# Pointwise product as the scan's last filler, two more pairs of input tiles by seven products

## The chip, the cores and the metric

One Trainium2 chip, one core. The metric is the device time of one execution in microseconds (us); lower is better. The chip's engines are called TensorE (PE in the profile; PEld is its weight load), VectorE (DVE), ScalarE (ACT), GpSimd (POOL) and SyncE (SP, which issues DMAs here).

## What is computed

One layer of a bidirectional sequence model, for 1024 positions of width 1024, in float32:

```
h = RMSNorm(x)
P = h @ W_in                     # 1024 x 8192 columns: GLU, q, v, z_f, z_b, og, g_a, g_b
a = GLU(P) -> depthwise conv (31) -> LayerNorm -> silu -> a @ W_pw      # 512 -> 1024
b = two gated scans (forward, backward) of q, v, z over 8 heads -> norm, gate -> @ W_o
x = x + W_out(sigmoid(g_a) * a + sigmoid(g_b) * b)
x = x + W_down(silu(dwconv3(h2 W_gate)) * (h2 W_up)),  h2 = RMSNorm(x)
return RMSNorm(x)
```

The change concerns the product `a @ W_pw` (the pointwise product), and four of the 64 column tiles of 128 that `h @ W_in` is made of.

## The kernel before, in words

Activations stand transposed: a tile has 128 channels on the partitions and 512 positions, half of the sequence. A tile of a product's output is 128 columns of the weight matrix times one half of the positions. Every factor is kept as a high and a low part (`split`, line 122: the cast to the high part is ScalarE's, the subtraction that leaves the low part is VectorE's, line 123), and a product of two such tiles takes three matmuls (`mm3`, lines 142 to 149: high by high, high by low, low by high). Weights are loaded into `wr` (2 buffers) and split into `wp` (4 pages); activations lie in `hx` (32 pages of 256 KB), and h itself takes 16 of those for each half of the positions.

There are three kinds of jobs. Each has a `prep`, which loads and splits its weights, and a `run`, which issues matmuls in pieces of six:

- `std_job` (line 250) computes one tile of 128 columns for one or both halves. With 8 contraction blocks, as for `h @ W_in`, that is 24 matmuls or 4 pieces a half; the pointwise product has 4 blocks, so 12 matmuls or 2 pieces a half.
- `duo_job` (line 267) takes two tiles together, first both on the first half, then both on the second.
- `pair_job` (line 281) computes two tiles of 128 columns over both halves by seven products of 12 matmuls in place of eight (Strassen's scheme). The sums of activations that it needs lie in `hx` and `hy` pages, the sums of weights are made from `wr` and `sw`, and part of its weight parts lie in `wq`, in the pool `p1`.

`run_jobs` (line 193) hands out the pieces of a list of jobs in order. The next job's `prep` is called when the one before has handed out its first pieces, and `later(n, do)` has something done n pieces later. A `Stream` wraps that: `fill(n)` issues n pieces at this point of the program. The program's order is therefore written by hand: what stands between two fills is issued between those pieces, on every engine.

The 56 tiles of `h @ W_in` that aren't the GLU's are in the list `todo`: per head q and og, then per head v, z_f, z_b, then the gates g_a and g_b. Their outputs are evicted by ScalarE and stored to DRAM scratch (`d_q`, `d_v`, `d_z`, `d_ga`, ...), from where later stages load them.

The stages around the change:

1. *Pairs* (lines 940 to 1010). The first 2 x NPAIRS = 34 entries of `todo` are computed as 17 pairs. They fill TensorE while VectorE makes the depthwise convolution (`conv_steps`, line 944) and then, once per half of the positions, the layer norm: it loads the convolved tiles from `d_cv` (line 978), sums over channels by matmuls with ones (lines 982, 518 and 528), and writes the normed, activated and split result to the tiles `ch` in the pool `gp0` (line 998).
2. *Pointwise product* (lines 1002 to 1010). After each half's layer norm 8 `std_job`s of that half are put into the list of jobs behind the pairs; 16 in all, 192 matmuls, reading `ch`. Each of the 16 loads and splits its weights anew. Then the pools `p1` and `gp0` are released.
3. *Scan* (lines 1015 to 1400). The pool `hp` takes their memory. `scan_inputs` (line 1053) loads z, q of a head and half and makes the gates on ScalarE and VectorE; `scan_base` (line 1077) forms cumulative products, with its tensor operations recorded by the helper at line 1042 (`DE`, `qF`, `kG`); `scan_levels`, `scan_states` and `scan_outputs` hold the scan's own, mostly small matmuls (lines 1162, 1174, 1188, 1245, 1295). Between them stand pieces of the 22 remaining entries of `todo` as filler, the stream `dense`: 21 pieces ahead of the first scan step, then `FILL` = 1.3 pieces between steps, and what is left after the last head in a fixed pattern (`left`, line 1403). The last filler job is a `duo_job` of the last two gate tiles. One v tile is loaded per head and half on SP (`load(d_v...)`), into the `tm` pages.
4. *Output of the scan.* `bm_loads` (line 1360) loads the scan's outputs from `d_bm` and splits them into `hx` pages, for the product with W_o. After that come the merge, W_out and the feed-forward part; the pointwise result is read back there from `d_a`.

Of the kernel before, what the change touches and what calls it, by code (L numbers as in the profile page):

```python
# [10 lines left out]
F32 = mybir.dt.float32  # L11
# [7 lines left out]
P = 128  # L19
FILL = 1.3  # L20
CONV_FILL = 1.6
NPAIRS = 17
LN_FILL = 6
LN_LAST = 12
GLU_FIRST = 4
# [21 lines left out]
def tile_hybrid_encoder(  # L47
# [22 lines left out]
    nc = tc.nc  # L70
    PSUM = bass.MemoryType.PSUM
    V, A, G, T = nc.vector, nc.scalar, nc.gpsimd, nc.tensor

    S, D = x.shape[1], x.shape[2]
    ND = D // P
    CW = conv_dw_w.shape[2]
    CK = conv_dw_w.shape[1]
    NCW = CW // P
# [20 lines left out]
    def bank(tag):  # L99
        return ps.tile([P, H], F32, tag=tag, name=nm(tag), bufs=BANKS[tag])  # L100

    def page(pool, tag, bufs, dt=F32):
        return pool.tile([P, H], dt, tag=tag, name=nm(tag), bufs=bufs)
# [4 lines left out]
    def ev():  # L108
        return page(mp, "ev", 3)

    def hx():
        return page(mp, "hx", 32, F32R)
# [9 lines left out]
    def split(hi, lo, src, eng, late=False):  # L122
        parts = A.copy(hi, src), eng.tensor_tensor(lo, src, hi.bitcast(F32), op=ALU.subtract)  # L123
        if late:
            for i in parts:
                pin(i)
        return hi, lo

    def w_cols(w, r0, nk, c0, cols=P):
        return w[0, r0 : r0 + nk * P, c0 : c0 + cols].rearrange("(k p) e -> p k e", p=P)  # L130

    def raw_w(src, nk):
        t = mp.tile([P, nk, P], F32, tag="wr", name=nm("wr"), bufs=2)
        nc.sync.dma_start(t, src)
        return t

    def w_page(nk, pool=None):
        if pool is None:
            return mp.tile([P, nk, P], F32R, tag="wp", name=nm("wp"), bufs=4)
        return pool.tile([P, nk, P], F32R, tag="wq", name=nm("wq"), bufs=3)  # L140

    def mm3(acc, w, act, k, first, last, again=False):


        whi, wlo = w
        ahi, alo = act
        T.matmul(acc, whi[:, k, :], ahi, start=first, stop=False, skip_group_check=again)  # L147
        T.matmul(acc, whi[:, k, :], alo, start=False, stop=False, skip_group_check=again)  # L148
        T.matmul(acc, wlo[:, k, :], ahi, start=False, stop=last, skip_group_check=again)  # L149
# [7 lines left out]
    def later(n, do):  # L157

        chores.append([n, do])

    def advance_chores(n=1):
        for c in list(chores):
            c[0] -= n
            if c[0] <= 0:
                chores.remove(c)
                c[1]()
# [26 lines left out]
    def run_jobs(jobs, lead=0, prime=0, first=None):  # L193


        live = collections.deque(maxlen=3)

        jobs = jobs if isinstance(jobs, collections.deque) else collections.deque(jobs)
        ready = collections.deque()

        def prepare(n):
            while jobs and len(ready) < n:
                prep, run = jobs.popleft()
                ready.append((run, prep()))
                live.append(ready[-1][1])

        def tick():
            for w in live:
                if isinstance(w, Weights):
                    w.tick()  # L210
            advance_chores()

        prepare(max(prime, 1))
        if prime:
            yield
        while ready:
            run, w = ready.popleft()
            pieces = run(w)
            for _ in itertools.islice(pieces, lead if first is None else first):
                tick()  # L220
                yield
            first = None
            prepare(1)
            for _ in pieces:
                tick()
                yield
            prepare(1)
# [21 lines left out]
    def std_job(src, nk, acts, evac, halves=(0, 1), step=2):  # L249


        def prep():
            raw = raw_w(src, nk)
            return split(w_page(nk), w_page(nk), raw, V)

        def run(w, halves=halves):
            for half in halves:
                acc = bank("mm")
                for k in range(nk):
                    mm3(acc, w, acts(k, half), k, k == 0, k == nk - 1)  # L260
                    if k % step == step - 1 or k == nk - 1:
                        yield
                evac(half, acc)

        return prep, run

    def duo_job(src0, src1, nk, acts, evac0, evac1):

        both = [std_job(src0, nk, acts, evac0), std_job(src1, nk, acts, evac1)]

        def prep():
            return [p() for p, _ in both]

        def run(w):
            for half in range(2):
                for (_, r), wi in zip(both, w):
                    yield from r(wi, (half,))

        return prep, run
# [197 lines left out]
    def scratch(name, *dims):  # L477
        if not dims:
            return dp.tile([P, H], F32, name=name)
        return [scratch(f"{name}_{i}", *dims[1:]) for i in range(dims[0])]  # L480

    d_h = scratch("d_h", ND, 2)
    d_cv = scratch("d_cv", NCW, 2)
    d_a = scratch("d_a", ND, 2)
    d_ga = scratch("d_ga", ND, 2)
    d_gb = scratch("d_gb", ND, 2)
# [12 lines left out]
    def in_cols(c0):  # L499
        return w_cols(w_in, 0, ND, c0)  # L500
# [212 lines left out]
    def store(dst, func=None):  # L713
        def evac(half, x0, x1=None, op=None):
            t = ev()
            if x1 is not None:
                V.tensor_tensor(t, x0, x1, op=op)  # L717
                x0 = t
            if func is not None:
                A.activation(t, x0, func)  # L720
            elif x1 is None:
                A.copy(t, x0)
            nc.sync.dma_start(dst[half], t)

        return evac
# [21 lines left out]
    def in_pair(n):  # L747
        (c0, e0), (c1, e1) = todo[2 * n], todo[2 * n + 1]
        evs = (e0, e1)
        return pair_job(  # L750
            in_cols(c0),
            in_cols(c1),
            NK2,
            lambda i: ht[i],
            p1,
            p1,
            lambda e, *quadrant: evs[e](*quadrant),
            first=n == 0 or n >= 12,
        )
# [179 lines left out]

    jobs = collections.deque(in_pair(n) for n in range(1, NPAIRS))  # L940
    jobs.appendleft((lambda: w_pair0, pair0[1]))
# [27 lines left out]
            V.tensor_tensor(o, o, t, op=ALU.add)  # L969
        return o  # L970

    pw_jobs = []
    for half in range(2):
        xs = []
        for j in range(NCW):
            if j % 2 == 0:
                both = p1.tile([P, 2, H], F32, tag="ca", name=nm("cx"), bufs=2)
            nc.sync.dma_start(both[:, j % 2, :], d_cv[j][half])
            xs.append(both[:, j % 2, :])
        s_pairs.fill(LN_FILL)  # L980
        mean = bank("ob")
        T.matmul(mean, ones_m, total(xs, tmp()), start=True, stop=True)
        for t in xs:
            V.scalar_tensor_tensor(t, mean, -1.0 / CW, t, op0=ALU.mult, op1=ALU.add)
        s_pairs.fill(LN_FILL)
        sqs = [tmp() for _ in xs]
        for sq, t in zip(sqs, xs):
            A.activation(sq, t, AF.Square)
        rstd = rstd_over_partitions(total(sqs, sqs[0]), CW, "ob", tmp())
        next(rstd)  # L990
        s_pairs.fill(5)
        rs = next(rstd)
        ca = []
        for j, xn in enumerate(xs):
            V.tensor_tensor(xn, xn, rs, op=ALU.mult)
            V.tensor_scalar(xn, xn, vec("lnw", j), vec("lnb", j), op0=ALU.mult, op1=ALU.add)
            A.activation(xn, xn, AF.Silu)
            both = gp0.tile([P, 2, H], F32R, tag="gl", name=nm("ch"), bufs=NCW)
            ca.append(split(both[:, 0, :], both[:, 1, :], xn, V))
        s_pairs.fill(LN_LAST)  # L1000
        at = 0
        while at < len(jobs) and jobs[at] in pw_jobs:
            at += 1
        for i in range(ND):
            job = std_job(
                w_cols(conv_pw_w, 0, NCW, i * P), NCW, lambda k, hf, ca=ca: ca[k], store(d_a[i]), (half,)
            )
            pw_jobs.append(job)
            jobs.insert(at + i, job)
    s_pairs.drain()  # L1010
    Stream(run_jobs(jobs)).drain()
    p1.release()
    gp0.release()


    rest = todo[2 * NPAIRS :]
    rest_jobs = [std_job(in_cols(c), ND, h_std, e) for c, e in rest[:-2]]
    (c0, e0), (c1, e1) = rest[-2:]
    rest_jobs.append(duo_job(in_cols(c0), in_cols(c1), ND, h_std, e0, e1))

    h12.clear()
    for k in range(NK2):
# [2 lines left out]
    dense = Stream(run_jobs(rest_jobs))  # L1025
# [343 lines left out]
    for h in range(NH):  # L1369
# [4 lines left out]
        for half in range(2):  # L1374
            i = 2 * h + half
# [24 lines left out]
            cur = ahead  # L1400
        pending = Stream(outputs(h, kept, Tt, Sf, Sb))

    left = 8 * (len(rest) - 2) + 16 - dense.count
    pending.fill(1)
    dense.fill(left - 20)
    pending.fill(1)
# [209 lines left out]
    gs, jobs = [], []  # L1616
# [183 lines left out]
```

## Time and profile before

| what | value |
|---|---|
| time, median of 3 runs (lowest, highest) | 1791.35 us (1791.15, 1793.52) |
| span of the profiled execution, first to last instruction | 1788.8 us |
| median less that span | 2.55 us |
| stages by start of TensorE's work in that trace: pairs | to 452.6 us |
| pointwise product | 452.6 to 500.6 us |
| filler ahead of the scan's first own matmul | 500.6 to 529.2 us |
| mean granted TensorE clock | 0.996 |

The profiled execution has no device time of its own beside the span; the span leaves out what the runs' times have around it. Times in the profile are counted from the span's start. In a row of the timeline the start, the duration, the engine, the source line, the operation, and output<-inputs by the program's names stand in this order; "x4" is a group of four, and a bracket tells the idle time before and what released it. A row "A <- B: 6.0, 7, 1.5" of the waits says that A stood 6.0 us for B in 7 waits, the longest 1.5.

### The profile page before, as it was taken

The numbers are of one execution on the slowest core, as the hardware profiler recorded it, in microseconds if no ns is written. First come the engines' busy times: TensorE is split into PE (matmuls) and PEld (weight loads), VectorE is DVE, ScalarE is ACT, GpSimd is POOL, SyncE is SP. The second block draws the span as 40 slices with busy tenths as digits, with TensorE's granted clock in tenths as the row PEclk, the third lists the DMA queues.
The fourth block names the chain that finished last, engine by engine and source line by source line (L and its number), as shares of the span: only waits on it lengthen the run. The fifth ranks groups of instructions, "written<-read, shape, count | busy, mean of one in ns | idle before, by whom it ended". The sixth has DMA issues, their size and how long they took to land.

```text
span 1788.8 us, 27583 instructions
## 1 busy us (share of the span) xinstructions
PE 1733.0 (97%) x10632; PEld 1416.7 (79%) x10638; DVE 1250.4 (70%) x1884; ACT 775.0 (43%) x1490; POOL 153.8 (9%) x168
## 2 busy tenths in 40 slices
PE   8989999999999999999999999999999999999997
PEld 6878877888777777777778888878888888888885
DVE  5599999746569999999645557667667667544455
ACT  7344333334555566655442245344344344422123
POOL 2201111000000000000000002011111111000000
PEclk9999999999999999999999999999999999999999
DMA  8657887743663433333257665567667665534233
GB/s 285 216 151 187 185 185 185 199 150 126 199 214 101 125 119 119 119 119 101 90 180 219 200 201 177 153 142 159 151 144 158 142 151 133 161 103 126 79 91 135
DMA packets 317705, 276.41 MB, mean 155 GB/s; under 512 B 14462, under 2 KB 242566, under 8 KB 317574
## 3 DMA queue, kind: packets, MB, share of 16 engines
q1 hardware_dynamic: 276406, 242.15, 43.1%
q0 software_dynamic: 41168, 32.51, 12.6%
q8 instruction: 83, 1.36, 0.3%
q14 instruction: 48, 0.39, 0.1%
HBM read 185.73 MB, written 72.61 MB: 144 GB/s over the span
## 4 chain that ended last, share of the span: by engine, by line
PE 65%; DVE 19%; DMA 5%; issue 4%; ACT 4%; POOL 1%; SPq 0%; POOLq 0%; DVEq 0%; ACTq 0%
PE mm L147 16%; PE mm L148 16%; PE mm L149 16%; PE sc L147 3%; PE sc L149 3%; PE sc L148 3%; DVE acc L955 2%; DVE kG L1042 2%; DVE DE L1042 2%; DVE qF L1042 2%; DVE wp L123 2%; PE tr L147 1%; PE tr L149 1%; PE tr L148 1%; DVE DE L1098 1%
## 5 line engine op out<-in xcount | busy, mean ns | idle before, releaser
L147 PE MATMUL mm<-hx,wp 128*128 128x512 f32 x1128 | 454.8, 403 | 9.8 <-DVE ev L717 4.3
L149 PE MATMUL mm<-hx,wp 128*128 128x512 f32 x1128 | 441.7, 392 | 1.9 <-DVE wp L123 1.9
L148 PE MATMUL mm<-hx,wp 128*128 128x512 f32 x1128 | 441.4, 391 | 0.0
L123 ACT CAST wp<-wr 128x1024 fp32r<-128x1024 f32 (+2 forms) x179 | 167.0, 934 | 359.6 <-PE mm L148 271.5
L147 PEld LDWEIGHTS mm<-hx,wp 128*128 128x128 f32 x1128 | 212.5, 188 | 55.7 <-DVE ev L717 6.7
L123 DVE TENSOR_TENSOR wp<-wr,wp 128x1024 fp32r<-128x1024 f32 (+2 forms) x177 | 191.4, 1082 | 90.4 <-ACT wp L123 90.1
L149 PEld LDWEIGHTS mm<-hx,wp 128*128 128x128 f32 x1128 | 212.6, 188 | 49.3 <-DVE wp L123 3.2
L148 PEld LDWEIGHTS mm<-hx,wp 128*128 128x128 f32 x1128 | 212.9, 189 | 40.4 <-issue 0.2
L955 DVE SCALAR_TENSOR_TENSOR acc<-gl,v_b,acc 128x1024 f32<-128x1024 f32 x120 | 149.0, 1277 | 0.5
L1651 DVE TENSOR_TENSOR xr<-mm,xr 128x512 f32<-128x512 f32 x48 | 33.2, 691 | 73.1 <-PE mm L149 73.1
L367 ACT COPY su<-mm 128x512 f32<-128x512 f32 x78 | 45.2, 579 | 62.5 <-PE mm L149 61.5
L123 ACT CAST wq<-sw 128x1024 fp32r<-128x1024 f32 x39 | 41.0, 1051 | 64.4 <-issue 28.6
L1500 DVE SCALAR_TENSOR_TENSOR tm<-gp,v_a,tm 128x512 f32<-128x512 f32 x88 | 65.9, 749 | 2.0
L147 PE MATMUL mm<-hy,wp 128*128 128x512 f32 x156 | 61.5, 394 | 1.4 <-ACT su L367 1.4
L148 PE MATMUL mm<-hy,wp 128*128 128x512 f32 x156 | 61.1, 392 | 0.0
L147 PE MATMUL sc<-hy,wq 128*128 128x512 f32 x156 | 61.1, 392 | 0.0
L149 PE MATMUL sc<-hy,wq 128*128 128x512 f32 x156 | 61.1, 391 | 0.0
L147 PE MATMUL tr<-hx,wp 128*128 128x512 f32 x156 | 60.8, 390 | 0.0
L149 PE MATMUL tr<-hx,wp 128*128 128x512 f32 x156 | 60.7, 389 | 0.0
L148 PE MATMUL tr<-hx,wp 128*128 128x512 f32 x156 | 60.7, 389 | 0.0
L148 PE MATMUL sc<-hy,wq 128*128 128x512 f32 x156 | 60.7, 389 | 0.0
L149 PE MATMUL mm<-hy,wp 128*128 128x512 f32 x156 | 60.6, 389 | 0.0
(368 smaller groups left out, 3467.6 us busy)
## 6 DMA issues: line engine op xcount, KB each, us to landing
wr<-in_w_in_dram SPq DMA_DIRECT2D x56, 512.0 KB, 4.7
wr<-in_ffn_w_up_dram SPq DMA_DIRECT2D x24, 512.0 KB, 4.9
sw<-in_ffn_w_up_dram SPq DMA_DIRECT2D x44, 256.0 KB, 3.0
d_g<-ft SPq DMA_DIRECT2D x44, 256.0 KB, 2.7
sw<-in_ffn_w_up_dram POOLq DMA_DIRECT2D x20, 512.0 KB, 8.3
sw<-in_w_in_dram SPq DMA_DIRECT2D x34, 256.0 KB, 3.2
d_z<-ev SPq DMA_DIRECT2D x32, 256.0 KB, 3.1
zi<-d_z SPq DMA_DIRECT2D x32, 256.0 KB, 3.2
```

Of the source, the lines that this page charges most:

```text
L123: parts = A.copy(hi, src), eng.tensor_tensor(lo, src, hi.bitcast(F32), op=ALU.subtract)
L147: T.matmul(acc, whi[:, k, :], ahi, start=first, stop=False, skip_group_check=again)
L148: T.matmul(acc, whi[:, k, :], alo, start=False, stop=False, skip_group_check=again)
L149: T.matmul(acc, wlo[:, k, :], ahi, start=False, stop=last, skip_group_check=again)
L367: A.copy(t, acc)
L955: V.scalar_tensor_tensor(acc, g[:, k : k + S], tap(k), acc, op0=ALU.mult, op1=ALU.add)
L1042: V.tensor_tensor(o, a, b, op=op)
L1098: V.reciprocal(ed(D, 7), ed(0, D + 7))
L1500: V.scalar_tensor_tensor(c, g[:, o + k : o + k + H], vec("fdw", k * NF + j), c, op0=ALU.mult, op1=ALU.add,)
L1651: V.tensor_tensor(xr[i][half], acc, xr[i][half], op=ALU.add)
```

## The change

- `NPAIRS` goes from 17 to 19: the entries 34 to 37 of `todo` (v of head 6 with z_f of head 6, z_b of head 6 with v of head 7) become two more pairs by seven products, ahead of the scan. In the scan's filler 18 entries of `todo` are left.
- The pointwise product isn't computed between pairs and scan any more. The split results of the layer norm are stored to a new DRAM scratch `d_ca` (16 stores of 256 KB, issued by SP).
- Behind the duo of the last two gate tiles the filler gets six pointwise `std_job`s over both halves and a `duo_job` of the last two columns, so each column's weights are loaded and split once. Their inputs are loaded from `d_ca` to 16 `hx` pages (`ca_loads`), eight pieces after the first of these jobs is prepared.
- `left` counts the pieces of the new list: 8 x 18 + 4 x 8 = 176 pieces in all, as 8 x 20 + 16 = 176 before.

```diff
-NPAIRS = 17
+NPAIRS = 19
...
+    d_ca = scratch("d_ca", NCW, 2, 2)
...
-    pw_jobs = []
...
-        ca = []
         for j, xn in enumerate(xs):
             V.tensor_tensor(xn, xn, rs, op=ALU.mult)
             V.tensor_scalar(xn, xn, vec("lnw", j), vec("lnb", j), op0=ALU.mult, op1=ALU.add)
             A.activation(xn, xn, AF.Silu)
             both = gp0.tile([P, 2, H], F32R, tag="gl", name=nm("ch"), bufs=NCW)
-            ca.append(split(both[:, 0, :], both[:, 1, :], xn, V))
+            for dst, part in zip(d_ca[j][half], split(both[:, 0, :], both[:, 1, :], xn, V)):
+                nc.sync.dma_start(dst, part.bitcast(F32))
         s_pairs.fill(LN_LAST)
-        at = 0
-        while at < len(jobs) and jobs[at] in pw_jobs:
-            at += 1
-        for i in range(ND):
-            job = std_job(
-                w_cols(conv_pw_w, 0, NCW, i * P), NCW, lambda k, hf, ca=ca: ca[k], store(d_a[i]), (half,)
-            )
-            pw_jobs.append(job)
-            jobs.insert(at + i, job)
     s_pairs.drain()
-    Stream(run_jobs(jobs)).drain()
...
     rest_jobs.append(duo_job(in_cols(c0), in_cols(c1), ND, h_std, e0, e1))
+    ca = [[None, None] for _ in range(NCW)]
+
+    def ca_loads(half):
+        for j in range(NCW):
+            parts = hx(), hx()
+            for part, src in zip(parts, d_ca[j][half]):
+                nc.sync.dma_start(part.bitcast(F32), src)
+            ca[j][half] = parts
+
+    def pw_col(i):
+        return w_cols(conv_pw_w, 0, NCW, i * P)
+
+    def ca_of(k, half):
+        return ca[k][half]
+
+    def pw_first():
+        prep, run = std_job(pw_col(0), NCW, ca_of, store(d_a[0]))
+
+        def loads():
+            later(8, lambda: [ca_loads(half) for half in range(2)])
+            return prep()
+
+        return loads, run
+
+    rest_jobs.append(pw_first())
+    rest_jobs += [std_job(pw_col(i), NCW, ca_of, store(d_a[i])) for i in range(1, ND - 2)]
+    rest_jobs.append(
+        duo_job(pw_col(ND - 2), pw_col(ND - 1), NCW, ca_of, store(d_a[ND - 2]), store(d_a[ND - 1]))
+    )
...
-    left = 8 * (len(rest) - 2) + 16 - dense.count
+    left = 8 * len(rest) + 4 * ND - dense.count
```

## The prediction

> **What bounds the kernel now.** First the page: the busy table and the chain of work that ended last.
>
> ```profile
> span 1788.8 us, 27583 instructions
> ...
> PE 1733.0 (97%) x10632; PEld 1416.7 (79%) x10638; DVE 1250.4 (70%) x1884; ACT 775.0 (43%) x1490; POOL 153.8 (9%) x168
> ...
> PE 65%; DVE 19%; DMA 5%; issue 4%; ACT 4%; POOL 1%; SPq 0%; POOLq 0%; DVEq 0%; ACTq 0%
> ```
>
> TensorE is busy for 97% of the span and holds 65% of the chain; VectorE holds 19%. So a matmul less is worth its time wherever TensorE is the one that sets the end, and the question is where VectorE does. The windows (length, then PE, PEld, DVE, ACT, POOL busy and counts, clock, DMA share, GB/s) answer that for the two stages that the change touches most: the pointwise product, and most of the scan.
>
> ```profile
> 452.40:500.40 48.00, 47.10 (x204) 37.17 (x203) 20.82 (x33) 26.09 (x49) 1.84 (x4) 1.00 0.68 217
> ...
> 529.20:850.00 320.80, 303.28 (x3938) 247.88 (x3944) 297.04 (x603) 187.49 (x457) 11.88 (x12) 1.00 0.37 115
> ```
>
> In the first VectorE is idle for more than half the time and TensorE is busy for 47.1 of 48.0 us: TensorE bounds. In the scan VectorE is busy 297.0 of 320.8 us (93%) and TensorE 303.3 (95%): both are near their limit, and who waits for whom is in the waits from 520 to 900 us (total, times, longest):
>
> ```profile
> PE ob L1162 <- DVE qF L1042: 6.0, 7, 1.5
> PE tr L1245 <- DVE kG L1042: 4.9, 7, 1.8
> ...
> DVE wp L123 <- ACT wp L123: 7.7, 4, 3.3
> ```
>
> TensorE waits 10.9 us for VectorE's qF and kG in these two groups alone. VectorE in turn stands 7.7 us in front of weight splits whose cast on ScalarE isn't there yet.
>
> **The change part by part.** The built programs' instruction lists, counted: matmuls 8921 before, 8897 after. 192 pointwise matmuls leave the place between pairs and scan; two pairs (7 products of 12) put 168 there. In the scan four tiles of 48 go and 192 pointwise ones come: the filler has 176 pieces before and after, and from the scan's first own matmul on TensorE's list is the same in length and order, only the operands differ.
>
> *The stretch before the scan.* A matmul's price isn't its duration. In the timeline (start, duration) the last product of the last pair, the first pointwise matmul and the first of the scan's filler read:
>
> ```profile
> 449.88 0.39 PE L147 MATMUL mm<-hx,wp 128*128 128x512 f32 x1
> ...
> 452.37 0.39 PE L149 MATMUL mm<-hx,wp 128*128 128x512 f32 x1
> 452.60 0.40 PE L147 MATMUL mm<-ch,wp 128*128 128x512 f32 x1
> ...
> 500.58 0.39 PE L147 MATMUL mm<-hx,wp 128*128 128x512 f32 x1
> ...
> 503.77 0.39 PE L149 MATMUL mm<-hx,wp 128*128 128x512 f32 x1
> ```
>
> Each lasts 0.39 us, but the next starts long before its end, so I count from start to start: 449.88 to 452.60 are the pair's 12, 0.2267 apart; 500.58 to 503.77 are 14 steps of the filler, 0.2279 apart. The pointwise stretch runs from 452.60 to 500.58, 47.98 us. Two layer-norm groups that stay lie in it:
>
> ```profile
> 453.76 0.39 PE L149 MATMUL mm<-ch,wp 128*128 128x512 f32 x1
> 453.99 0.95 PE L528 MATMUL ob<-ones_m,tm 128*128 128x1 f32 x8
> 454.80 0.48 PE L147 MATMUL mm<-ch,wp 128*128 128x512 f32 x1
> ...
> 461.62 0.40 PE L149 MATMUL mm<-ch,wp 128*128 128x512 f32 x1
> ...
> 462.94 0.39 PE L148 MATMUL mm<-ch,wp 128*128 128x512 f32 x1
> ```
>
> Five pointwise steps, 452.60 to 453.76, are 0.232 apart. 453.76 to 454.80 is 1.04 instead of 0.23, so L528 costs 0.81; 461.62 to 462.94 holds the other group and is 1.32 instead of two steps, 0.46, so that costs 0.86; together 1.7. The 192 matmuls account for 192 x 0.232 = 44.5, the groups for 1.7, and 1.8 are waits of the pointwise product's own. After: 168 x 0.2267 + 1.7 = 39.8, a gain of **8.2 us**. Were the pairs spaced as the pointwise product is, and as much waiting found elsewhere, it would be 24 x 0.232 = 5.6. I take 8.2, because the pair's own rows are nearest, and keep 5.6 as the other end.
>
> The Trainium skill (TensorE: Matmul & The Clock Gate, "Back-to-back issue gap") gives a sustained 131 ns per matmul of 512 columns, and 216 for an isolated one; by 131 the 24 matmuls would be worth 3.1 us. The rows above show 227 to 232 in sustained streams, so the measurement decides.
>
> Beside it, hidden: VectorE's work on the two pairs' weights. By the instruction lists a pair brings ten VectorE instructions; the sixteen half-size pointwise splits go. The full split in the scan has this row (count, busy, mean ns, idle before):
>
> ```profile
> L123 DVE TENSOR_TENSOR wp<-wr,wp 128x1024 fp32r<-128x1024 f32 x18 | 21.9, 1218 | 7.7 <-ACT wp L123 7.7
> ```
>
> Twenty at no more than 1.22 us are 24.4; sixteen at half of it, an estimate, are 9.8. The 20.8 us of VectorE become 35.4 at most, in a stretch of 39.8: still under it. Cover gone, what is over would be paid in full.
>
> The sixteen stores of conv results stand on SP ahead of the second half's layer-norm loads. What a 256 KB transfer takes of SP, and the slack of the layer norm, show in these rows:
>
> ```profile
> 923.53 2.73 SPq L116 DMA_DIRECT2D tm<-d_bm  x4
> ...
> 928.73 2.56 ACT L123 CAST hx<-tm 128x512 fp32r<-128x512 f32 x4 [3.98 <-DMA tm<-d_bm]
> ```
>
> ```profile
> 445.99 2.48 DVE L984 SCALAR_TENSOR_TENSOR cx<-ob,cx 128x512 f32<-128x512 f32 x4 [6.32 <-PE ob L982]
> ```
>
> Four take 2.73 us to issue, so the first half's eight take 5.5. VectorE, done with the sum, waits 6.3 us until TensorE comes to it. Nothing is lost; with that slack gone each further store would cost its 0.7.
>
> *The start of the scan.* Its first inputs wait for memory that the last pair frees, in place of the pointwise product's.
>
> ```profile
> 529.25 0.73 PE L1174 MATMUL sc<-Qh,Kh 128*32 128x32 f32 x62
> ...
> 533.31 0.46 PE L1162 MATMUL ob<-qF,A 128*32 128x32 f32 x32 [1.46 <-DVE qF L1042]
> ```
>
> Before, 21 pieces of filler cover the chain from 500.58 until the first own matmul at 529.25, which shows no wait; a later one waits 1.46. After, the pair's pool is free when its sixth product ends, one product (12 x 0.2267 = 2.7 us) before the filler starts. So the chain may start up to 2.7 us earlier against TensorE, or no earlier, if an eviction holds it. I take 0.7, half of the 1.46 that can go; ends 0 and 2.7.
>
> *The filler in the scan.* Spacing: nothing, as filler and pointwise rows differ by 0.0041 us (192 x 0.0041 = 0.8 as the other end). Splits: eight of half the size for four. Their work is the same; four handshakes with ScalarE are more. Eighteen full splits stood 7.7 us in all, 0.43 each: 4 x 0.43 = 1.7. I take **1.7 us** lost, with 0 and 12 as ends (all eight at nearly half of the longest wait, 3.3). Eight more evictions lie in ScalarE's idle time (187.5 us busy of 320.8).
>
> *The reloads.* They take the sixteen pages of h's first half once the last gate pair has read them, and the first pointwise matmul comes eight pieces later. In the clock of before these places are:
>
> ```profile
> 816.17 0.39 PE L149 MATMUL mm<-hx,wp 128*128 128x512 f32 x1
> ...
> 842.55 0.48 PE L147 MATMUL mm<-hx,wp 128*128 128x512 f32 x1
> ```
>
> That is 26 us of cover. The nearest row is the reload of four pages at 923.53 above, on the same queue: used from 928.73, 5.2 us after the first issue, and no cast waits for the next one. Sixteen are four such groups, 21 us: hidden, with 5 over. Behind them on SP stand a gate store and the next two v loads; nothing wants those in these 21 us.
>
> *The tail.* The last pointwise cast stands on ScalarE inside the last output's scaling, for which TensorE already waits:
>
> ```profile
> 908.42 1.21 PE L1321 MATMUL tr<-ident,tm 128*128 128x128 f32 x4 [2.11 <-ACT tm L1314]
> ```
>
> One cast of a 128x512 tile is 0.64 us (2.56 over 4 at 928.73). I take 0.5 lost, ends 0 and 2. Later stages have the same lists.
>
> **Sum:** -8.2 - 0.7 + 1.7 + 0.5 = -6.7 us against the span of 1788.8, so 1782.1. The runs' median is 1791.35, 2.55 above this span; that stays around it. Forecast **1784.6 us**.
>
> **The rivals.** *The scan takes the gain.* VectorE is at 93%; were four of the new splits to stand 1.9 us each (7.7 over the 4 waits), 7.7 instead of 1.7 is lost: 1784.6 + 6.0 = 1790.6. Against it: most of the eighteen filler splits stood behind nothing.
>
> *The reloads are late (the slower end).* If each waits for the one before,
>
> ```profile
> zi<-d_z SPq DMA_DIRECT2D x32, 256.0 KB, 3.2
> ```
>
> gives 16 x 3.2 us from issue to landing, 51 us against 26 of cover. TensorE would stand 25 us at its first pointwise matmul: 1784.6 + 25 = 1809.6. It decides from 33 us for the sixteen, when 7 us of stall eat the gain. The row of four speaks against it. The Trainium skill (DMA: Bandwidth & Descriptors, "Anatomy of one DMA") says that a semaphore wait is served by the issuing sequencer before dispatch: a reload that waits for its page would hold all of SP. No run here shows it yet; by it the v loads would be held as well, one more stall at the same place.
>
> *More than the sum.* The lead of 2.7 us stays through the scan, and no split stands: -8.2 - 2.7 = -10.9, 1780.4.
>
> *It doesn't do what it says:* excluded by the count. But the pairs could stall, and the gain be 5.6: 1787.2, still faster.
>
> **How the numbers follow.** Forecast, with its own ends 1781 and 1787.7, 0.62; more 0.10; the scan takes the gain 0.15; reloads late or another stall of that kind 0.13. What a measurement of this kernel can tell from no change is about 0.2%, 3.6 us, so faster means below 1787.8: 0.62 + 0.10 = 0.72; within 0.15; slower 0.13. The range 1780 to 1792 reaches from the case of more to that of the scan with the tail at its end of 2 (1790.6 + 1.5), and leaves out the late reloads.
>
> **What would show it.** Right: a first scan matmul near 521 (529.25 - 8.2), spacing 0.227 up to it, no wait over 1 us on TensorE from 452 to 521, no DMA named as releaser at the first pointwise matmul in the scan, and VectorE's waits for wp near 9.4 us (7.7 + 1.7). Wrong: TensorE waiting for hx from d_ca; VectorE's waits for wp above 14; a longer wait at 908's transpose; or a scan as long as before plus what the start gained.

## The result, and the profile after

| | before | after |
|---|---|---|
| median of 4 runs (lowest, highest) | 1792.43 us (1791.15, 1794.43) | 1783.76 us (1781.09, 1784.11) |
| span of the profiled execution | 1788.8 us | 1782.3 us |

After over before is 0.9939, 95% interval 0.9922 to 0.9956: faster, by 8.7 us in these medians and by 6.6 in the two traces. The page of the kernel after, in the three lines that stand for those shown of before:

```profile
span 1782.3 us, 27603 instructions
...
PE 1730.3 (97%) x10614; PEld 1415.1 (79%) x10614; DVE 1257.5 (71%) x1892; ACT 773.8 (43%) x1486; POOL 153.7 (9%) x168
...
PE 65%; DVE 16%; DMA 7%; issue 6%; ACT 4%; POOL 1%; SPq 0%; POOLq 0%; DVEq 0%; ACTq 0%
```

The shares hardly move, and they can't: 6.6 us of 1789 are 0.4%. What moved is read by places. Behind the change every line number is 19 higher than before (L1174 is L1193, L1295 is L1314, L1321 is L1340); a few ahead of it are one higher (L528 is L529). I take five matmuls that both traces have, and compare what lies between them; the rows of after are quoted below, as far as before's stand in the prediction.

| stretch of TensorE, us | before | after | change |
|---|---|---|---|
| start to the layer norm's mean, second half (L982) | 444.93 | 445.60 | +0.7 |
| from there to its second sum (L528) | 9.06 | 9.54 | +0.5 |
| from there to the scan's first own matmul (L1174) | 75.26 | 67.21 | **-8.0** |
| scan, to its last state matmul (L1254, `sc<-v,kT`) | 364.41 | 361.69 | **-2.7** |
| tail, to the first matmul of W_out (`mm<-mg,wp`) | 114.23 | 117.31 | **+3.1** |
| the rest, to the end of the span | 780.94 | 780.91 | 0.0 |

The first row holds the same matmuls in both kernels: over nine executions of the changed kernel and its variants with 19 pairs this point lies between 444.6 and 449.0, so 0.7 lies within the scatter of executions. The third row is firm: in the same nine it is 67.21 to 67.29. The six rows add up to the spans, 1788.83 and 1782.26 us. The windows of after, 453.6 to 493.7 the pairs' part up to the filler, then the scan over the same length as shown of before:

```profile
453.60:493.70 40.10, 40.10 (x181) 32.90 (x180) 22.97 (x33) 18.76 (x32) 2.46 (x6) 1.00 0.65 210
522.30:843.10 320.80, 305.42 (x4042) 248.94 (x4041) 296.60 (x607) 188.90 (x461) 11.91 (x12) 1.00 0.39 125
```

TensorE is busy for all of the 40.1 us in which the two pairs stand, where the pointwise stretch took 48.0 with 47.1 busy; VectorE has 23.0 us of work there. In the timeline:

```profile
450.92 0.50 PE L147 MATMUL mm<-hx,wp 128*128 128x512 f32 x1 [0.21 <-DVE ev L718]
...
453.78 0.39 PE L147 MATMUL mm<-hx,wp 128*128 128x512 f32 x1
...
455.14 0.61 PE L529 MATMUL ob<-ones_m,tm 128*128 128x1 f32 x5
...
493.69 0.39 PE L147 MATMUL mm<-hx,wp 128*128 128x512 f32 x1
...
522.35 0.73 PE L1193 MATMUL sc<-Qh,Kh 128*32 128x32 f32 x62
...
525.55 0.46 PE L1181 MATMUL ob<-qF,A 128*32 128x32 f32 x32 [0.58 <-DVE qF L1061]
```

The last pair of before ends ahead of 453.78, and the filler starts at 493.69; that is 39.9 us against 47.98. The wait in front of 450.92 is new (it costs 0.37 beside the spacing). The scan's first matmul is 6.9 us earlier than at 529.25, and the wait for qF behind it fell from 1.46 to 0.58. The waits of the scan (here 513 to 892 us):

```profile
DVE wp L123 <- ACT wp L123: 11.3, 5, 3.9
...
PE ob L1181 <- DVE qF L1061: 5.7, 8, 0.9
...
PE tr L1264 <- DVE kG L1061: 4.7, 6, 1.8
```

VectorE stands 3.6 us more for casts than before, and TensorE 0.5 less for VectorE's qF and kG in these groups. How both go together is what the run with full-width splits below tells. The tail, TensorE in the timeline, then the windows of the same place:

```profile
898.79 0.48 PE L1340 MATMUL tr<-ident,tm 128*128 128x128 f32 x1 [2.09 <-ACT tm L1333]
899.61 1.06 PE L1340 MATMUL tr<-ident,tm 128*128 128x128 f32 x3 [0.34 <-ACT tm L1333]
...
901.32 0.63 PE L149 MATMUL mm<-hx,wp 128*128 128x512 f32 x1
901.74 0.63 PE L147 MATMUL mm<-hx,wp 128*128 128x512 f32 x1
```

```profile
898.70:905.60 6.90, 6.47 (x17) 4.80 (x18) 2.82 (x4) 4.11 (x12) 0.00 (x0) 0.51 0.61 207
905.60:913.80 8.20, 8.20 (x37) 6.73 (x36) 3.58 (x5) 5.52 (x10) 0.00 (x0) 1.00 0.68 205
```

The transposes of the last outputs wait 2.09 us, as they did before, then 0.34 more between the first and the others, and eleven steps of the matmuls behind them are 0.43 us instead of 0.23: the granted clock (the third column from the end) is 0.51 there. Before, the clock was 1.00 through the same place (908.4 to 916.0 us). From the first transpose to the next group of them, 48 matmuls on, it takes 3.1 us more than before, all that the tail lost here: 0.6 up to the first matmul and 2.5 in the slow steps.

### The profile page after: what moved, and what is told of

It reads as the page before. It is cut to its first block, busy times and chain, and to the rows that moved or that the text cites. A ratio compares the mean times of both kernels' runs of the same rounds, so it can differ in the third digit from the quotient of the medians.

```text
span 1782.3 us, 27603 instructions
## 1 busy us (share of the span) xinstructions
PE 1730.3 (97%) x10614; PEld 1415.1 (79%) x10614; DVE 1257.5 (71%) x1892; ACT 773.8 (43%) x1486; POOL 153.7 (9%) x168
## 3 DMA queue, kind: packets, MB, share of 16 engines
q8 instruction: 83, 1.36, 0.3%
## 4 chain that ended last, share of the span: by engine, by line
PE 65%; DVE 16%; DMA 7%; issue 6%; ACT 4%; POOL 1%; SPq 0%; POOLq 0%; DVEq 0%; ACTq 0%
PE mm L147 16%; PE mm L148 16%; PE mm L149 16%; PE sc L147 3%; PE sc L149 3%; PE sc L148 3%; DVE acc L956 3%; DMA sw<-in_w_in_dram 3%; DVE kG L1061 2%; DVE wp L123 2%; DVE qF L1061 2%; DVE DE L1061 1%; PE tr L149 1%; PE tr L147 1%; PE tr L148 1%
## 5 line engine op out<-in xcount | busy, mean ns | idle before, releaser
L147 PE MATMUL mm<-hx,wp 128*128 128x512 f32 x1144 | 462.5, 404 | 9.9 <-DVE ev L718 4.7
L149 PE MATMUL mm<-hx,wp 128*128 128x512 f32 x1144 | 449.5, 393 | 1.4 <-DVE wp L123 1.4
L148 PE MATMUL mm<-hx,wp 128*128 128x512 f32 x1144 | 448.9, 392 | 0.0
L123 ACT CAST wp<-wr 128x1024 fp32r<-128x1024 f32 (+2 forms) x171 | 162.1, 949 | 352.9 <-PE mm L148 227.4
L147 PEld LDWEIGHTS mm<-hx,wp 128*128 128x128 f32 x1144 | 216.6, 189 | 57.0 <-DVE ev L718 7.6
L149 PEld LDWEIGHTS mm<-hx,wp 128*128 128x128 f32 x1144 | 216.3, 189 | 49.5 <-DVE wp L123 2.5
L123 DVE TENSOR_TENSOR wp<-wr,wp 128x1024 fp32r<-128x1024 f32 (+2 forms) x169 | 185.8, 1100 | 92.0 <-ACT wp L123 80.1
L148 PEld LDWEIGHTS mm<-hx,wp 128*128 128x128 f32 x1144 | 216.7, 189 | 41.1 <-issue 0.2
L147 PE MATMUL mm<-hy,wp 128*128 128x512 f32 x164 | 64.7, 395 | 2.0 <-ACT su L367 2.0
L147 PE MATMUL sc<-hy,wq 128*128 128x512 f32 x164 | 64.6, 394 | 0.0
L148 PE MATMUL mm<-hy,wp 128*128 128x512 f32 x164 | 64.3, 392 | 0.0
L149 PE MATMUL sc<-hy,wq 128*128 128x512 f32 x164 | 64.2, 391 | 0.0
L147 PE MATMUL tr<-hx,wp 128*128 128x512 f32 x164 | 63.9, 390 | 0.0
L149 PE MATMUL tr<-hx,wp 128*128 128x512 f32 x164 | 63.8, 389 | 0.0
L148 PE MATMUL tr<-hx,wp 128*128 128x512 f32 x164 | 63.8, 389 | 0.0
L148 PE MATMUL sc<-hy,wq 128*128 128x512 f32 x164 | 63.8, 389 | 0.0
L149 PE MATMUL mm<-hy,wp 128*128 128x512 f32 x164 | 63.7, 389 | 0.0
```

## The experiments

All ratios are to the kernel before, run beside it on the same chip, with their 95% intervals; the changed kernel stands at 0.9939 (0.9922 to 0.9956). Since these overlap for many, the stretches of the table above in us, read from each run's trace, carry more:

| run | ratio | median us | L528 to scan | scan | tail |
|---|---|---|---|---|---|
| changed kernel | 0.9939 | 1783.76 | 67.21 | 361.69 | 117.31 |
| move only (17 pairs) | 1.0028 (1.0016 to 1.004) | 1800.45 | | 369.58 | 153.84 |
| one more pair (18) | 0.9947 (0.9931 to 0.9962) | 1786.29 | | 364.55 | 132.59 |
| 1.2 pieces between steps | 0.9977 (0.9965 to 0.9988) | 1789.75 | 67.29 | 358.95 | 125.75 |
| two idle matmuls | 0.9930 (0.9915 to 0.9944) | 1783.75 | 67.22 | 362.90 | 116.35 |
| full-width splits | 0.9952 (0.9939 to 0.9966) | 1784.87 | 67.22 | 363.44 | 116.47 |
| later loads, not held | 0.9931 (0.9918 to 0.9945) | 1781.53 | 67.24 | 362.30 | 116.37 |
| 18 pairs, 1.4 pieces | 0.9939 (0.9923 to 0.9955) | 1783.10 | | 374.75 | 120.12 |
| 18 pairs, 1.35 pieces | 0.9946 (0.9933 to 0.9958) | 1784.21 | | 370.18 | 125.08 |
| later loads, held | 0.9961 (0.9948 to 0.9973) | 1787.04 | 67.21 | 364.47 | 116.47 |
| last split in hx pages | 0.9940 (0.9924 to 0.9956) | 1782.39 | 67.22 | 361.88 | 114.28 |
| two pieces earlier | 0.9935 (0.9920 to 0.9951) | 1783.97 | 67.23 | 361.60 | 116.25 |
| both | 0.9925 (0.9913 to 0.9936) | 1780.96 | 67.23 | 362.41 | 114.21 |

**The move without further pairs.**

```diff
-NPAIRS = 19
+NPAIRS = 17
```

> Only the move of the pointwise product, no further pairs (17 pairs as before, the filler has 208 pieces). Theory: TensorE's count sets the price, so the two pairs taken back cost 24 x 0.2267 = 5.4 us against the changed kernel; but the 32 pieces more are left for the last outputs, where the changed kernel has only 10 pieces, stands idle for 2.4 us (2.09 + 0.34) before the transposes and then runs 12 matmuls at twice the spacing (2.4 us): -4.8. Together about 1784.4 us, and TensorE with no wait over 1 us at these transposes. Rival, the pairs are the whole gain and the end of the scan costs nothing: 5.4 us above the changed kernel at least, 1789 to 1792.

Measured 1.0028 of before: slower than either kernel. Both theories missed it. The tail did what was expected: 32 pieces of 1.36 us (6 x 0.2267) are 43.5 us, and it grew by 36.5 only, so 7 us of pauses and slow steps went. But the first scan matmul came at 493.65, while two pairs less should put it 38.1 us before 522.35, at 484.3. The 9.4 us are gaps that open on TensorE: with the pointwise product gone and no pair in its place, nothing covers the layer norm of the second half (its squares, `tm`), the splits of h's second half that the filler reads (`hx`), and the first head's Kh. The waits from 440 to 494 us:

```profile
PE ob L519 <- ACT tm L518: 3.9, 1, 3.9
PE sc L1193 <- DVE Kh L1064: 1.3, 1, 1.3
PE mm L148 <- DVE hx L123: 1.1, 3, 0.7
```

A fourth wait, 0.6 us for ScalarE's part of the `hx` splits, makes 6.9 in all, and from 458 to 468 us, behind the longest of them, the granted clock is 0.83. So the two edits of the change aren't two independent gains: the pairs are the cover that the moved product had been.

**One more pair instead of two.**

```diff
-NPAIRS = 19
+NPAIRS = 18
```

> One more pair instead of two, pointwise product moved (192 pieces of filler). Theory: 12 matmuls more, +2.7 us, and 26 pieces left for the last outputs, -4.8: about 1781.7 us, faster than the changed kernel. Rival, the idle time at the end of the scan is hidden or reappears elsewhere: 1786.5 us.

The first scan matmul came at 504.19, 18.2 us earlier than with two (84 x 0.2267 = 19.0 by the spacing), and the tail, with 16 pieces more, grew by 15.3 where they are 21.8: the pauses at the transposes are gone, 6.5 us. But the scan took 2.9 more, and the time is the changed kernel's or a little above it. This is the rival's case, 1786.3 us where it said 1786.5: the gain in the tail came back elsewhere and didn't pay for the pair. Why the scan took longer isn't traced.

**Less filler in the scan.** The changed kernel has 10 of 176 pieces left when the last scan step is done; with 1.2 between steps it has 21.

```diff
-FILL = 1.3
+FILL = 1.2
```

> The changed kernel with 1.2 instead of 1.3 pieces of filler between scan steps, so that about 21 pieces are left for the last outputs instead of 10; no work is added or taken. Theory: the 2.4 us of idle and the 2.4 us of doubled spacing at the last transposes go, about 1779 us. Rival, VectorE bounds the scan, so each piece taken out of it shows as a TensorE wait for qF or kG of the same length there: 11 x 1.4 = 15 us of new waits against what the end gives, 1784 or more.

The rival held in its time, 1789.75. The 11 pieces, 15 us of TensorE, made the scan only 2.7 us shorter, and the tail 8.4 longer. The windows of the scan in this run, in the changed kernel, and in the run with 18 pairs and 1.4 pieces, in that order (each is a row of its own trace):

```profile
522.30:881.33 359.03, 333.79 (x4436) 270.91 (x4435) 321.68 (x662) 207.05 (x512) 13.72 (x14) 1.00 0.37 120
```

```profile
522.30:884.04 361.74, 345.69 (x4502) 282.36 (x4502) 322.22 (x664) 210.31 (x520) 13.74 (x14) 1.00 0.39 124
```

```profile
503.73:878.50 374.77, 361.04 (x4564) 295.71 (x4568) 327.27 (x666) 212.09 (x523) 14.76 (x14) 1.00 0.39 124
```

TensorE is busy for 93%, 95.6% and 96.3% of the three scans. From 1.2 to 1.3 TensorE's busy time rises by 11.9 us and the scan by 2.7, so most of these pieces fill what would be waits. The waits themselves are not where the rival put them. Those for VectorE's qF and kG, in three groups, are 13.6 us in the scan of both kernels. What grows with less filler is the waiting for ScalarE's copies, in this run and then in the changed kernel:

```profile
PE sc L1273 <- ACT kT L1266: 4.2, 5, 1.3
PE ob L1181 <- ACT A L1179: 3.0, 4, 1.1
PE sc L1181 <- ACT A L1179: 1.0, 3, 0.5
```

```profile
PE sc L1273 <- ACT kT L1266: 1.0, 2, 0.6
```

That VectorE alone bounds the scan is therefore not shown: the filler covers VectorE and ScalarE together. It is nearly free up to about 1.3 pieces between steps.

**More filler in the scan, with one more pair instead of two.**

```diff
-NPAIRS = 19
+NPAIRS = 18
-FILL = 1.3
+FILL = 1.4     # f2: 1.35
```

> One more pair instead of two, pointwise product moved, and 1.4 instead of 1.3 pieces of filler between scan steps: 192 pieces, of which 15 are left for the last outputs. Theory: VectorE bounds the scan, since 11 pieces less there (15 us of TensorE) shortened it by 2.7 us only; so 11 pieces more cost it 5 us at most (a third of their 15 us), while the tail is 15 us shorter than with 1.3: 10 us below the kernel with one pair and 1.3, about 1776, the fastest so far. Rival, at 95% busy TensorE bounds it already: the scan grows by the full 15 us, 1786.

> As the run with 1.4, with 1.35 pieces of filler between scan steps, 20 or 21 pieces left for the last outputs. Theory (VectorE bounds the scan): half of the effect, about 1781. Rival (TensorE bounds it): 1786, as with 1.3.

Missed: 1.4 gave 0.9939 and 1.35 gave 0.9946, both within the interval of the changed kernel, and their times, 1783.1 and 1784.2, lie between theory and rival. Against 18 pairs with 1.3, the scan rose by 10.2 us for 11 pieces (15 us) and the tail fell by 12.5; with 1.35 it was 5.6 and 7.5. From 1.2 to 1.3 (with 19 pairs) a piece in the scan costs a fifth of its time, from 1.3 on (with 18) two thirds. Neither version is better than the changed kernel.

**Two idle matmuls in the pause.**

```diff
...
+            if h == NH - 1 and half == 0:
+                idle = bank("sc")
+                for _ in range(2):
+                    T.matmul(idle, ones_m, Sf[1].rearrange("p c e -> p (c e)"), start=True, stop=True)
             b = bank("tr")
```

> The changed kernel with two matmuls added whose result nobody reads (ones by a state tile, into a free bank, 0.86 us each) behind the last 12 filler matmuls ahead of the last outputs' transposes, where TensorE waits 2.09 us. Theory, the doubled spacing after it (0.427 instead of 0.227 us for 12 matmuls, granted clock 0.50) comes from that pause: spacing 0.227 throughout, clock 1.00, 2.4 us less, about 1781.4. Rival, it comes from something else at this place (sixteen loads of bm, DMA share 0.80): spacing 0.427 stays, 1784.

Half of it held. The clock is 1.00 behind the transposes (the windows of this run):

```profile
902.30:913.30 11.00, 11.00 (x49) 9.08 (x50) 5.27 (x8) 7.37 (x16) 0.00 (x0) 1.00 0.83 259
```

and the 48 matmuls behind the transposes take 11.0 us instead of 13.5. One execution doesn't show that the missing pause is the reason: the run with held loads below has the pause and no slow step either. And the tail fell by 1.0 only. The waits of this run from 895 to 1003 us show one that the changed kernel doesn't have:

```profile
PE tr L1344 <- ACT tm L1333: 0.9, 2, 0.5
PE mm L149 <- DVE wp L123: 0.8, 1, 0.8
```

A weight split for the product with W_o is late, and 1.6 us more come back between the last transposes and the first matmul of W_out (88.75 us against 87.17). So without the slow steps 1.0 of the 3.1 us that the tail lost comes back; the rest stands behind another delay.

**Full-width splits of the pointwise weights.** The eight weight tiles are loaded twice over and split at 1024 columns; the matmuls use half of it.

```diff
+    wide = []
...
+            if acts in wide:
+                raw = mp.tile([P, ND, P], F32, tag="wr", name=nm("wr"), bufs=2)
+                for ks in (slice(0, nk), slice(nk, ND)):
+                    nc.sync.dma_start(raw[:, ks], src)
+                return split(w_page(ND), w_page(ND), raw, V)
...
+    wide.append(ca_of)
```

> The changed kernel with the eight pointwise weight tiles loaded twice over and split at the full width of 1024 columns (half of it unused), as the four tiles that they replaced were; the matmuls are the same. Theory: the changed kernel ran the pointwise part of the scan 1.9 us faster than before (the lead went from 7.7 to 9.6 us between 830 and 896) because a split there holds VectorE 0.69 instead of 1.22 us ahead of qF and kG; with full-size splits these waits come back and the time is about 1.9 us above the changed kernel's, 1786. Rival, the gain there comes from the earlier start or from fewer loads on SP: the lead of 9.6 at the last scan step stays within 0.3 us and the time is the changed kernel's, 1784.

The theory held in the scan, which took 1.75 us more; the medians, 1784.87 and 1783.76, can't tell the two kernels apart. The same two matmuls in three traces, the first ahead of the pointwise part of the scan, the second at its end; before, after, and this run:

```profile
830.36 0.33 PE L1174 MATMUL sc<-Qh,Kh 128*32 128x32 f32 x16
...
895.93 0.27 PE L1295 MATMUL ob<-v,S 128*128 128x128 f32 x1
```

```profile
822.72 0.27 PE L1193 MATMUL sc<-Qh,Kh 128*32 128x32 f32 x8
...
886.31 0.27 PE L1314 MATMUL ob<-v,S 128*128 128x128 f32 x1
```

```profile
822.75 0.29 PE L1202 MATMUL sc<-Qh,Kh 128*32 128x32 f32 x11
...
887.93 0.27 PE L1323 MATMUL ob<-v,S 128*128 128x128 f32 x1
```

The stretch is 65.57 us before, 63.59 after, 65.18 here: of the 2.0 us that the changed kernel wins in it, 1.6 go with the size of the splits. TensorE's waits for VectorE at this place show it too; before (820 to 896 us), after (814 to 886), and this run (814 to 896):

```profile
PE ob L1162 <- DVE qF L1042: 0.8, 1, 0.8
PE sc L1188 <- DVE qF L1042: 0.6, 1, 0.6
PE tr L1245 <- DVE kG L1042: 0.6, 2, 0.4
```

```profile
PE ob L1181 <- DVE qF L1061: 0.7, 1, 0.7
PE tr L1264 <- DVE kG L1061: 0.4, 1, 0.4
```

```profile
PE ob L1190 <- DVE qF L1070: 1.6, 2, 1.0
PE sc L1216 <- DVE qF L1070: 0.5, 1, 0.5
PE tr L1273 <- DVE kG L1070: 0.3, 1, 0.3
```

They are 2.0, 1.1 and 2.4 us: 1.3 of the 1.6 stand in them. The casts on ScalarE and the loads grow in this run as well; VectorE's part is not separated from theirs. The rest, 0.4, isn't traced further.

**Later reloads, not held.**

```diff
-            later(8, lambda: [ca_loads(half) for half in range(2)])
+            later(16, lambda: [ca_loads(half) for half in range(2)])
```

> The changed kernel with the sixteen reloads issued 16 instead of 8 filler pieces after the first pointwise job is prepared, so right ahead of their first use. Theory: they go out one every 0.65 us and land in 3.6, so TensorE waits some 4 us at the first pointwise matmul and up to 2 more for the following ones: 4 to 6 us above the changed kernel, 1788 to 1790, and with the 26 us of cover there they are hidden with more than 10 to spare. Rival, each waits for the one before: eight of the first half take 26 us, 1809 or more. Second rival, TensorE has slack there because VectorE bounds the scan: within 1 us of the changed kernel.

It gave 0.9931, no slower. But the trace shows that the edit didn't do what it says: the first loads went out at 806.28 us, where the changed kernel's go out at 806.67, because the planner (the part of the program's builder that orders the transfers) puts a load to where its page comes free, whatever its place in the source. The last went out at 820.9, against 816.4. So this run says nothing on the cover, and it is one more execution of nearly the same program: its difference from 0.9939 is scatter.

**Later reloads, held in program order.**

```diff
-            later(8, lambda: [ca_loads(half) for half in range(2)])
+            later(16, lambda: [ca_loads(half) for half in range(2)])
...
-                nc.sync.dma_start(part.bitcast(F32), src)
+                pin(nc.sync.dma_start(part.bitcast(F32), src))
```

> The changed kernel with the sixteen reloads held in program order right ahead of their first use (16 pieces after the first pointwise job is prepared; without the hold the planner had put them back to where their pages come free). In SP's list they now stand behind the last store but one of the gates, an estimated 20 us later than in the changed kernel, with some 7 us of cover instead of 27. Theory, the queue takes one every 0.65 us and the first land after 3.6: TensorE waits 0 to 4 us in all at the first pointwise matmuls, 1784 to 1788. Rival, each waits for the one before, 3.2 us a piece: the first half's eight take 26 us, so TensorE waits some 19 us there, 1800 or more.

SP's row of the loads in the changed kernel, then in this run:

```profile
806.67 10.14 SPq L1016 DMA_DIRECT2D hx<-d_ca  x16
```

```profile
831.65 10.89 SPq L1016 DMA_DIRECT2D hx<-d_ca  x16
```

The theory held. Sixteen go out in 10 to 11 us either way, so one in 0.63 to 0.68: they are issued one behind another without waiting for one another to land, which takes 4.6 us at the median in the changed kernel and 5.5 here. (The 3.6 in the expectations is the median of the sixteen stores to d_ca and the sixteen reloads together.) Here they start 6 us ahead of the first matmul that reads them (837.77), there 27. The waits of this run, TensorE's weight loads from 830 to 860 us and its matmuls from 800 to 1010:

```profile
PEld mm L148 <- DMA hx<-d_ca: 2.3, 5, 0.5
PEld mm L147 <- DMA hx<-d_ca: 1.4, 4, 0.3
```

```profile
PE mm L148 <- DMA hx<-d_ca: 0.6, 3, 0.2
```

The scan took 2.8 us more and the ratio is 0.9961. With 6 us of cover the reloads cost some 3 us. With 27 us of it they cost nothing: in the changed kernel's trace no wait of TensorE names d_ca.

**The last split in hx pages.**

```diff
+    prep6, run6 = duo_job(
...
+    def last_prep():
+        raws = [raw_w(pw_col(i), NCW) for i in (ND - 2, ND - 1)]
+        spare = [hx().rearrange("p (k e) -> p k e", k=NCW) for _ in range(2)]
+        return [
+            split(w_page(NCW), w_page(NCW), raws[0], V),
+            split(spare[0], spare[1], raws[1], V),
+        ]
+
+    rest_jobs.append((last_prep, run6))
```

> The changed kernel with the last pointwise column's two weight parts in free hx pages instead of wp pages, so that their split doesn't wait for a page and its cast on ScalarE stands ahead of the last outputs' scaling instead of inside it. Theory: the cast is what the tail lost; the wait of 0.34 us between the transposes goes, the pause comes back to that of before (2.1 us), the doubled spacing behind it goes or gets short, and the tail (from the last scan step's last matmul to the first with mg) falls from 116.4 to 117.3 to about 114.2 us: 1781. Rival, the pause of 2.1 us alone makes the doubled spacing: the tail stays over 116.

The theory held in the trace: the tail is 114.28, before's length. The ratio, 0.9940, can't tell it from the changed kernel. ScalarE in the changed kernel, then in this run:

```profile
898.34 0.40 ACT L1333 ACTIVATE tm<-tm,ors 128x128 f32<-128x128 f32 x1 [2.03 <-POOL ors L511]
898.65 0.60 ACT L123 CAST wp<-wr 128x512 fp32r<-128x512 f32 x1
899.16 2.15 ACT L1333 ACTIVATE tm<-tm,ors 128x128 f32<-128x128 f32 x7
```

```profile
899.15 1.57 ACT L1343 ACTIVATE tm<-tm,ors 128x128 f32<-128x128 f32 x5 [2.03 <-POOL ors L511]
```

The pointwise product's last cast waits for a wp page, and in the changed kernel it stands between the first scaling and the other seven; with pages of its own it stands ahead of them. TensorE's only wait at the place is then again 2.08 us, and the spacing behind it 0.23.

**Two pieces earlier, and both.** Four of the ten left pieces ahead of the transposes instead of two; in the last run together with the hx pages.

```diff
-    dense.fill(left - 20)
+    dense.fill(left - 18)
```

> The changed kernel with four instead of two of the ten left filler pieces ahead of the last outputs' transposes, six instead of eight behind them; no work is added. Theory: two pieces are 2.7 us of TensorE and fill the pause of 2.4; no doubled spacing, and the tail falls by 2.4 to 4 us, about 1781. Rival, the pause moves behind the transposes, where six pieces no longer cover the splits of bm: TensorE waits for hx or wp there and the time is the changed kernel's, 1784.

> Both: the last column's weight parts in hx pages and four of the ten pieces ahead of the transposes. Theory: no pause at the transposes and no cast inside the scaling, 1780 or a little less, the fastest version. Rival: what is won at the transposes comes back as waits for bm or weights in the product with W_o, 1783 to 1784.

Alone it is the rival's case: the pause is gone, the clock 1.00, and TensorE waits 3.0 us for weight splits of the product with W_o instead (the waits from 895 to 1003 us):

```profile
PE mm L147 <- ACT wp L123: 1.9, 2, 1.0
PE mm L149 <- DVE wp L123: 1.1, 2, 0.5
```

The tail is 116.25. With both it is 114.21, the same as with the hx pages alone, and 1.5 us of waits for wp stand where the pause was. At 0.9925 it has the lowest ratio of all runs, and beats the kernel before clearly. Against the changed kernel it is 2.8 us less in medians that were not taken side by side, and the intervals overlap; in the stretches, the tail's 3.1 us are all that it surely has over the changed kernel.

## Why the prediction was right, point by point

- **The stretch before the scan, -8.2.** Right: -8.0 from L528 to the scan, and TensorE busy for all of the pairs' 40.1 us. The pairs run at 0.2267 a matmul, and nothing new waits in them. Counting from start to start gave this; durations (0.39 each) would have given 24 x 0.39 = 9.4 for the matmuls alone, where they are worth 5.4 to 5.6. Not foreseen: 0.5 us just ahead, most of it at 450.92, where TensorE waits for an eviction by VectorE. VectorE has the next pair's weights beside it there; that this makes the eviction late was not tried.
- **VectorE's work on the weights, hidden.** Right: 23.0 of 40.1 us. The 35.4 at most were too high by 12.
- **The start of the scan, -0.7.** Right: the wait for qF fell by 0.9, and the lead (how much earlier than before a matmul of the scan starts) grew from 6.9 to 7.8 us at that wait and was 7.6 at 822.7.
- **The filler in the scan, +1.7.** This step failed, in its sign: "Eighteen full splits stood 7.7 us in all, 0.43 each: 4 x 0.43 = 1.7." VectorE's waits for casts did grow, from 7.7 to 11.3 (forecast 9.4), but TensorE's waits for qF and kG didn't grow with them. What TensorE pays is how long one split holds VectorE ahead of qF and kG, and a split of 0.69 us holds it for shorter at a time than one of 1.22, though eight of the first are more in sum than four of the second (5.5 against 4.9): the pointwise part of the scan was 2.0 us shorter, and the run with full-width splits took 1.6 of them back. That it is VectorE's share of the split, and not ScalarE's cast ahead of it, fits the waits and isn't separated. I had the row for it (TensorE's waits for qF and kG) and priced another one.
- **The reloads, hidden.** Right, with more to spare than worked out: 10.1 us to issue sixteen and 4.6 to landing (their median in the trace) against the 21 that I scaled from four, whose 5.2 us were mostly the first one's landing. The v loads behind them on SP went out at 820.30, where 814.33 less the lead would be 806.7, and no wait of TensorE names them. The rival by which each waits for the one before is excluded by the held run.
- **The tail, +0.5.** The mechanism was right (the last pointwise cast inside the last outputs' scaling), the size wrong: +3.1 in the changed kernel's trace and +2.1 to 2.2 in three other executions with the same tail (full-width splits, both later loads). I priced the cast by its own 0.6 us. What it set off is the doubled spacing in some executions, and late splits for W_o in others: the tail is long in all six kernels with 19 pairs and 1.3 pieces whose last split is on wp pages, 116.2 to 117.3, and short in the two without, 114.2 and 114.3. That the late cast holds a page which W_o's first splits want is my reading of why it comes back as waits for wp; what is shown is that the tail has before's length when this split is on hx pages.
- **The sum, -6.7.** Measured by the traces -6.57 in span, in parts -8.05 + 0.48 - 2.72 + 3.08 + 0.67 - 0.03. Two errors, of 3.7 us the one way in the filler and 2.6 the other way in the tail, nearly cancel: that the total is better than its terms is luck.
- **The 2.55 us around the span.** Too much by 0.8. In every run whose time and span are both known they are 1.7 to 1.9 us apart (the changed kernel's profiled run: 1784.03 and 1782.3). The profiled execution of before was faster than its median, by an estimate 1790.6 us (1788.8 + 1.8), and that is most of the difference between -6.6 in the traces and -8.7 in the medians. With 1.8 the sum would have been 1783.9; measured was 1783.76.
- **The rivals.** "The scan takes the gain" is refuted: the scan gave 2.7 more. "More than the sum" had that much from the scan, by another way (the lead of 2.7 from the start), and nothing lost in the tail. What no part of the prediction had: the pairs are not only fewer matmuls, they cover the layer norm and the filler's first splits; without them the move loses.

By the Trainium skill (TensorE: Matmul & The Clock Gate, "Wait — 56ns, not 53.3ns?") matmuls of 512 columns start 426.7 ns apart while the array is cold and about 216 when it is warm. The trace agrees on the first, 0.427 us in the slow stretch; warm, it shows 0.227, and the prices here go by that.

## What to carry to other kernels

Price a matmul from start to start in its own stream, not by its duration, and a stage by what waits last in it: here matmuls ahead of the scan cost nearly all of their time, and a piece of filler inside it a fifth or two thirds, depending on how much was there already. When work is moved away, ask what it had been covering: the same move without something in its place was slower than doing nothing. And a small cast that stands behind a page is to be priced by what it stands in front of, not by its own length.

## What the runs showed of the hardware

- After a pause of 2.09 us on TensorE and four transposes with a second wait among them, the granted clock was 0.51 for 6.9 us and 11 matmuls started 0.43 us apart. In other executions with that tail it was 5 and 7 steps (full-width splits, later loads not held) and none (held loads); before, and with the hx pages, a pause of 2.11 and 2.08 us with the transposes in one go left the clock at 1.00. So it doesn't hang on the length of the pause alone. From the end of the last matmul ahead of the pause to the first behind the transposes it is 3.04 and 3.07 us in the two executions with the transposes in one go, and 3.56 to 4.07 in the other four, three of them with slow steps; what else decides was not tried further. The Trainium skill (TensorE: Matmul & The Clock Gate, "What's actually happening") has the clock set by a free-running window of about 3.4 us; slow stretches of 0 to 11 steps at one place of the program agree with that, and no run here measures the window.
- The same code takes different time in its early part: up to the layer norm's second mean the traces of nearly identical programs differ by 4.4 us (444.6 to 449.0), while stretches on TensorE's own pace repeat within 0.1 us. A change of 0.5% is better read from such stretches than from one span.
